# Full-height products and spread-by-transposition in a hybrid encoder block on one core

## The chip, the core and the metric

One NeuronCore of one Trainium2 chip runs the whole program; the other cores are idle. The metric is the time of one execution on the device in microseconds (us), as the median of repeated runs. PE is TensorE, DVE is VectorE, ACT is ScalarE, POOL is GpSimd, SP is the queue from which nearly all DMAs are issued.

## The reference, cut to what matters

One encoder layer over 16 meta tokens and 512 tokens of width 1024, in float32:

```
u    = rms_norm(h);  proj = u @ w_in              # r,k,v | low-rank wd, ad, gd | q,k,v | gates A, B
A:   z = centred_shift(p);  decay = exp(-exp(-softplus(-(w0 + tanh(wd) @ w2)) - 0.5))
     a = sigmoid(a0 + ad @ a2);  g = sigmoid(gd) @ g2
     kk = (k * k_k) / max(norm(k * k_k per head), 1e-12)          # "key norm"
     scan per direction: S = S*w + (S @ -kk) x (kk*a) + v x k';  y = S @ r
     y = group_norm(y per head) * lnx_g + lnx_b + bonus;  out = y * g   # "group norm"
B:   grouped attention: softmax(q_norm_rope @ k_norm_rope) @ v
h   += (sigmoid(A) * (y_a @ wba) + sigmoid(B) * (y_b @ wbb)) @ w_out
h   += relu(rms_norm(h) @ w_ff1)^2 @ w_ff2;   out = rms_norm(h)
```

## The kernel before

Activations lie with channels on the 128 partitions and tokens along the row. A float32 product is usually made of three products of rounded pieces: `mm3` (lines 132 to 134) multiplies hi with hi, hi with lo and lo with hi, where hi is the value rounded to the faster product format and lo the rest. Weights come by `wblock` (lines 121 to 128): a DMA of 512 KB, a cast on ACT (`whi`), a subtraction on DVE (`wlo`).

The stages, in order of time: (1) up to 75 us, the projections of the low-rank inputs, the normalisation of the tokens and of the attention's keys; (2) 75 to 152 us, the queries (lines 132 to 134 into `mm`), the tables of decay, in-context rate and gate for all head pairs (lines 498 to 549, the `rw` banks), and the first r,k,v projections (`project_rkv`, lines 191 and 192); (3) 155 to about 590 us, for four head pairs `hp`: preparation (`prepare`, which begins with `key_norm`), inversion of blocks (`invert`), the serial scan over nine chunks (`chain`) and `finish` with the group norm, with the rest of the projections and the gates as filler, and from about 443 us on the attention (`attend`) among them; (4) the branch projections, the output projection and the feed-forward part to the end.

The order of the instructions on each engine is drawn up at build time by a planner that simulates the program with its own costs (`schedule_with_timeline_sim=True`); `tc.issue_after` holds the stage of the tables behind a given product, and `run` mixes the parts of stage 3 by turns with a fixed pace of fillers. The engines then run their lists in that order. A change of operations can therefore change the order too.

Four kinds of place matter here.

- Products over fewer than 128 rows. The tables of decay and rate multiply a stacked operand (`wds[d]`, `ads[d]`: 64 rows of hi and 64 rows of lo) once with 128 rows of hi weights, `hh[d]` (lines 506 and 537), and then the 64 hi rows with 64 rows of lo weights (lines 507 and 538). For the 16 meta tokens lines 525 and 526 multiply plain float32 operands over 16 and 64 rows. Line 598 spreads the key norm of the meta tokens over 16 rows. Line 1078 adds the meta tokens' part of the attention's output over 48 rows, once for each half of the queries of each head. Line 546 is the gate's last product, over 96 rows.
- Spreads. A factor per token lies along the partitions and is needed along the row: it is copied to a full 128x128 tile (`rx`) and multiplied with the identity, in plain float32. Each such product stands as two PE records in the trace. This is done for the token norm (line 269, and 272 for the meta tokens), for the key norm (603) and the group norm (920) of each head pair, and for the norm before the feed-forward part (1223), four products of 128 columns each time. The attention's probabilities are turned by `pe.transpose` (line 1063), one record each.
- `constants()` (lines 304 to 327): casts on ACT and subtractions on POOL that make `hh`, `lo` and the gate's weights.
- The tile `sg` (line 508) in three buffers: DVE adds the bias (509), ACT applies the sigmoid (510) and casts (513), POOL subtracts (514). The one for the meta tokens (`i == 4`) is kept until the last product of line 525.

Of the kernel before, what the change touches and what calls it, by code (L numbers as in the profile page):

```python
# [7 lines left out]
F32R = mybir.dt.float32r  # L8
# [6 lines left out]
P = 128  # L15
# [34 lines left out]
def block_kernel(tc, A, out, dbg=None):  # L50
# [34 lines left out]
    with root:  # L85
# [20 lines left out]
        DC_C0, DC_KKH, DC_KAH, DC_KAB, DC_A0H, DC_RKH = 0, 16, 20, 24, 28, 0  # L106
        tmpc = T(cp, [P, 16])
        rkh = T(cp, [P, 4])
# [42 lines left out]
        with ph1:  # L151
# [22 lines left out]
            def whole(steps):  # L174
                while True:
                    try:
                        next(steps)
                    except StopIteration as e:
                        return e.value
# [46 lines left out]
            with ExitStack() as es:  # L226
# [15 lines left out]
                sy.dma_start(cst, A["cst"])  # L242
                ps12 = whole(project_steps(first, raw))
                g.tensor_tensor(tmpc, par[:, PC_MU0:PC_MU0 + 16], par[:, PC_MU1:PC_MU1 + 16], op=ALU.add)
                g.tensor_scalar(der[:, 0:16], tmpc, -1.0, 1.0, op0=ALU.mult, op1=ALU.add)
# [22 lines left out]
                for i in range(4):  # L268
                    pe.matmul(ps[:, i * P:(i + 1) * P], rx[:, i], ident, start=True, stop=True)
                s.copy(RT[:, NM:L], ps)  # L270
                ps = T(chp, [P, 512], tag="yp", bufs=1)
                pe.matmul(ps[:, 0:NM], rx[:, 4], ident[:, 0:NM], start=True, stop=True)
                s.copy(RT[:, 0:NM], ps[:, 0:NM])
# [31 lines left out]
                def constants():  # L305

                    c = {}
                    trr = T(wpy, [P, 2, P], F32R)
                    g.tensor_copy(trr, tri)
                    c["tri"] = trr  # L310
                    for n, t in (("w2", w2), ("a2", a2)):
                        hh = [T(wpy, [P, 512], F32R) for _ in range(2)]
                        lo = T(wpy, [P, 512], F32R)
                        for d in range(2):
                            for o in (d, 1 - d):
                                s.copy(hh[d][HF[o]], t[HF[d]])
                            g.tensor_tensor(lo[HF[d]], t[HF[d]], hh[d][HF[d]], op=ALU.subtract)
                        c[n] = hh, lo
                    gh, gl = T(wpy, [P, 512], F32R), T(wpy, [P, 512], F32R)
                    s.copy(gh, gw0)  # L320
                    g.tensor_tensor(gl, gw0, gh, op=ALU.subtract)
                    gs = T(wpy, [96, 512], F32R)
                    for x in (0, 2):
                        s.copy(gs[32 * x:32 * x + 32], gw1)
                    v.tensor_tensor(gs[32:64], gw1, gs[0:32], op=ALU.subtract)
                    c["gw"] = gh, gl, gs
                    return c
# [159 lines left out]
                v.tensor_tensor(sl, sgd0, sh, op=ALU.subtract)  # L487
                sst = T(wpz, [96, SEQ], F32R)
                for x in range(2):
                    s.copy(sst[32 * x:32 * x + 32], sgd1)  # L490
                v.tensor_tensor(sst[64:96], sgd1, sst[0:32], op=ALU.subtract)
                keys_values(tk_, qkg, identr)
# [5 lines left out]
                with tc.issue_after(started):  # L498
                    sgs = {}
                    for d in range(2):  # L500
                        for i in range(4 if d else 5):
# [4 lines left out]
                            pe.matmul(ps[0:n, :], wds[d][:, c - 48:c - 48 + n], hh[d], start=True, stop=False)  # L506
                            pe.matmul(ps[0:n, :], wds[d][HF[d], c - 48:c - 48 + n], lo[HF[d]], start=False, stop=True)
                            sg = T(wpy, [P, 512], tag="sg", bufs=3)
                            v.tensor_tensor(sg[0:n, :], ps[0:n, :], w0b[0:n, d, :], op=ALU.add)
# [7 lines left out]
                    for d in range(2):  # L517
                        for hp in range(NHP):
# [4 lines left out]
                            if d == 0:  # L523
                                pm = bank()
                                pe.matmul(pm[:, 0:NM], sgs[0, 4][0:NM, hc], tri[0:NM, 0, 0:NM], start=True, stop=True)
                                pe.matmul(pm[:, 16:32], a2[0:64, hc], adz[0:64, 48:64], start=True, stop=True)
                                v.tensor_copy(lo_[:, 0, 0:NM], pm[:, 0:NM])
                                s.activation(lo_[:, 1, 0:NM], pm[:, 16:32], AF.Tanh, scale=0.5, bias=ab)
# [8 lines left out]
                            pe.matmul(ps, hh[d][:, hc], ads[d][:, NM:L], start=True, stop=False)  # L537
                            pe.matmul(ps, lo[HF[d], hc], ads[d][HF[d], NM:L], start=False, stop=True)
                            s.activation(lo_[:, 1, NM:L], ps, AF.Tanh, scale=0.5, bias=ab)
# [13 lines left out]
            gtp = pool(ph1a, "gt1", side="right")  # L553
            rp = pool(ph1, "rw")
            def load_rkv(hp):
                zs = []
                for x in range(3):
                    z = T(zp, [P, 576], tag="z", bufs=ZB)
                    g.memset(z[:, 0:48], 0.0)
                    sy.dma_start(z[:, 48:576], z_d[hp, x])  # L560
                    zs.append(z)
                return zs
# [14 lines left out]
            def key_norm(hp, zk):  # L577
# [13 lines left out]
                rx = G()  # L591
                rxm = T(rp, [NM, P], tag="rxm", bufs=1)
                v.tensor_copy(rx[:, 0:512].rearrange("p (a b) -> p a b", b=64), rn[:, 0:8].unsqueeze(2).broadcast_to([P, 8, 64]))
                v.tensor_copy(rxm.rearrange("p (a b) -> p a b", b=64), rn[0:NM, 8:10].unsqueeze(2).broadcast_to([NM, 2, 64]))
                kkh = G("k")
                g.memset(kkh[:, 0:48], 0.0)
                ps = bank()
                pe.matmul(ps[:, 0:NM], rxm, ident[0:NM, 0:NM], start=True, stop=True)
                v.scalar_tensor_tensor(kkh[:, 48:64], zk[:, 48:64], dcol(DC_KKH + hp), ps[:, 0:NM],
                                       op0=ALU.mult, op1=ALU.mult)  # L600
                ps = bank()
                for i in range(4):
                    pe.matmul(ps[:, i * P:(i + 1) * P], rx[:, i * P:(i + 1) * P], ident, start=True, stop=True)
                v.scalar_tensor_tensor(kkh[:, 64:576], zk[:, 64:576], dcol(DC_KKH + hp), ps,
# [293 lines left out]
            def finish(hp, sh):  # L898
# [20 lines left out]
                for i in range(4):  # L919
                    pe.matmul(ps[:, i * P:(i + 1) * P], rx[:, i * P:(i + 1) * P], ident, start=True, stop=True)  # L920
                yield
# [99 lines left out]

            vm = T(ap_, [48, 2, P], F32R)
            pms = [T(ap_, [48, 256], F32R) for _ in range(2)]
            for part, t in ((0, khh), (1, kll)):
# [3 lines left out]
            lpp = pool(aes, "aloop", side="right")  # L1028
            zz = T(lpp, [P, 256], tag="yo", bufs=2)[0:48]
            g.memset(zz, 0.0)  # L1030
# [102 lines left out]
        with ExitStack() as es:  # L1133
# [88 lines left out]
            for i in range(4):  # L1222
                pe.matmul(ps[:, i * P:(i + 1) * P], rx[:, i, :], ident, start=True, stop=True)
            s.copy(RS, ps)
# [152 lines left out]
```

## Time and profile before

| | |
|---|---|
| time, median of 3 runs | 1050.72 us (1048.79 to 1052.95) |
| the profiled execution, its own time | 1051.4 us |
| span in its profile | 1049.6 us |
| PE busy / weight loads (PEld) | 994.9 us (95%) / 816.1 us (78%) |
| DVE / ACT / POOL busy | 592.2 (56%) / 434.4 (41%) / 185.9 us (18%) |
| granted PE clock, mean | 0.968 of full speed |
| DMA | 107.25 MB, mean 102 GB/s |

The span is the profiled stretch; about 1.8 us of that execution's time lie outside it. Busy shares are averages over very different stages. A PE record lasts longer than the step from its start to the next record's start, since products overlap in the array; what a product costs the stream is read from starts.

### The profile page before, as it was taken

To read this page: it belongs to the slowest core of one execution; us is meant where nothing else is said; L and a number is where in the kernel's file an instruction comes from. 1 tells how busy PE (TensorE), PEld (TensorE's weight loads), DVE (VectorE), ACT (ScalarE), POOL (GpSimd) and SP (SyncE) were. 2 spreads that over 40 slices of the span, in tenths; PEclk is the share of its full clock that TensorE was granted. 3 is DMA by queue.
4 is the path that set the end of the run, shared out by engine and by line. 5 is a ranking of instruction groups with operands and counts; after the bars stand their busy time and mean duration, and the time that the engine had idled before them with its cause. 6 is when DMAs were issued, how large, how long until landed. Compare 5 with 4: busy or idle time off the path is not lost.

```text
span 1049.6 us, 17962 instructions
## 1 busy us (share of the span) xinstructions
PE 994.9 (95%) x7208; PEld 816.1 (78%) x7208; DVE 592.2 (56%) x1084; ACT 434.4 (41%) x802; POOL 185.9 (18%) x373
## 2 busy tenths in 40 slices
PE   7799989989999899989989999999999999999996
PEld 7778978877767676767777788888888888888885
DVE  4967647756663737396977566455555552123123
ACT  6676434424322524275788533343332232113112
POOL 1266411411411132112311123000000000001001
PEclk9999999999989899886999999999999999999999
DMA  9233662232222211510010284222233332322322
GB/s 348 70 113 86 197 239 71 72 117 100 80 93 92 82 62 62 174 42 11 12 32 21 82 269 132 83 86 95 98 101 101 101 109 92 101 92 89 101 96 85
DMA packets 45508, 107.25 MB, mean 102 GB/s; under 512 B 5264, under 2 KB 12736, under 8 KB 45424
## 3 DMA queue, kind: packets, MB, share of 16 engines
q1 hardware_dynamic: 44848, 105.05, 30.7%
q8 instruction: 57, 0.93, 0.4%
q10 hardware_dynamic: 576, 1.05, 0.3%
q14 instruction: 27, 0.22, 0.1%
HBM read 87.54 MB, written 18.54 MB: 101 GB/s over the span
## 4 chain that ended last, share of the span: by engine, by line
PE 81%; DVE 10%; ACT 4%; issue 2%; DMA 2%; POOL 0%; SPq 0%; ACTq 0%; DVEq 0%; POOLq 0%
PE f L134 8%; PE f L133 8%; PE f L132 8%; PE t L132 6%; PE t L133 6%; PE t L134 6%; PE mm L132 5%; PE mm L133 4%; PE mm L134 4%; PE mm L191 4%; PE mm L192 3%; PE rw L705 2%; PE rw L813 2%; PE yp L869 1%; PE xu L847 1%
## 5 line engine op out<-in xcount | busy, mean ns | idle before, releaser
L126 ACT CAST whi<-wraw 128x1024 fp32r<-128x1024 f32 x118 | 123.7, 1050 | 321.9 <-PE f L134 76.8
L127 DVE TENSOR_TENSOR wlo<-wraw,whi 128x1024 fp32r<-128x1024 f32 x118 | 148.6, 1260 | 183.8 <-ACT whi L126 183.4
L191 PE MATMUL mm<-t,whi 128*128 128x264 f32 x240 | 70.0, 309 | 7.6 <-ACT t L239 7.5
L132 PE MATMUL f<-t,whi 128*128 128x512 f32 x184 | 72.0, 392 | 0.0
L133 PE MATMUL f<-t,whi 128*128 128x512 f32 x184 | 71.7, 390 | 0.0
L134 PE MATMUL f<-t,wlo 128*128 128x512 f32 x184 | 70.9, 390 | 0.0
L192 PE MATMUL mm<-t,whi 128*128 128x264 f32 x240 | 67.7, 299 | 0.0
L133 PE MATMUL t<-wlo,t 128*128 128x512 f32 x160 | 63.4, 396 | 0.0
L133 PE MATMUL f<-wlo,t 128*128 128x512 f32 x160 | 63.3, 396 | 0.0
L134 PE MATMUL f<-whi,t 128*128 128x512 f32 x160 | 63.3, 396 | 0.0
L134 PE MATMUL t<-whi,t 128*128 128x512 f32 x160 | 63.3, 395 | 0.0
L132 PE MATMUL mm<-t,whi 128*128 128x512 f32 x128 | 58.1, 454 | 0.0
L191 PEld LDWEIGHTS mm<-t,whi 128*128 128x128 f32 x240 | 47.9, 199 | 10.8 <-ACT t L239 7.5
L132 PE MATMUL t<-whi,t 128*128 128x512 f32 x160 | 54.7, 397 | 0.0
L132 PE MATMUL f<-whi,t 128*128 128x512 f32 x160 | 53.9, 395 | 0.0
L132 PE MATMUL t<-t,whi 128*128 128x512 f32 x136 | 53.2, 393 | 0.2 <-ACT whi L126 0.2
L134 PE MATMUL t<-t,wlo 128*128 128x512 f32 x136 | 53.0, 391 | 0.0
L133 PE MATMUL t<-t,whi 128*128 128x512 f32 x136 | 52.6, 389 | 0.0
L133 PE MATMUL mm<-t,whi 128*128 128x512 f32 x128 | 52.2, 408 | 0.0
L134 PE MATMUL mm<-t,wlo 128*128 128x512 f32 x128 | 52.0, 406 | 0.0
L1266 POOL TENSOR_TENSOR t<-t,t 128x512 f32<-128x512 f32 x4 | 5.1, 1302 | 261.0 <-DVE t L1263 261.0
L192 PEld LDWEIGHTS mm<-t,whi 128*128 128x128 f32 x240 | 47.9, 200 | 1.5 <-issue 1.4
(338 smaller groups left out, 2372.6 us busy)
## 6 DMA issues: line engine op xcount, KB each, us to landing
wraw<-in_w SPq DMA_DIRECT2D x32, 512.0 KB, 3.4
wraw<-in_w2f SPq DMA_DIRECT2D x32, 512.0 KB, 3.4
wraw<-in_wrk SPq DMA_DIRECT2D x16, 512.0 KB, 3.9
wraw<-in_wg SPq DMA_DIRECT2D x16, 512.0 KB, 3.7
t<-gt SPq DMA_DIRECT2D x16, 256.0 KB, 2.0
gt<-t SPq DMA_DIRECT2D x16, 256.0 KB, 3.3
wraw<-in_wo SPq DMA_DIRECT2D x8, 512.0 KB, 3.4
g<-t SPq DMA_DIRECT2D x12, 256.0 KB, 3.4
```

Of the source, the lines that this page charges most:

```text
L126: s.copy(hi, raw)
L127: v.tensor_tensor(lo, raw, hi, op=ALU.subtract)
L132: pe.matmul(o, ah, bh, start=first, stop=False)
L133: pe.matmul(o, ah, bl, start=False, stop=False)
L134: pe.matmul(o, al, bh, start=False, stop=last)
L191: pe.matmul(pa, wt[:, w], ut[:, k, 0:264], start=first, stop=last)
L192: pe.matmul(pb, wt[:, w], ut[:, k, 264:528], start=first, stop=last)
L705: pe.matmul(ps[:, c - a, :, :], bkh(h, c), xr[HR[h], h:h + 2, c, :], start=True, stop=True)
L813: pe.matmul(ps[HR[h], cc], hs[HR[h], cc], cur[HR[h], cc], start=True, stop=True)
L847: pe.matmul(X[HR[h], j], ps[d]["xr"][:, 2 * h, c, :], svu[:, c, h, :], start=True, stop=True)
L869: pe.matmul(yp[HR[h], j], svu[:, c, h, :], ps[d]["rl"][:, h, c, :], start=False, stop=last and j == 1)
L1266: (v if half else g).tensor_tensor(o[:, i, cols], h1[:, i, cols], fg[:, cols], op=ALU.mult)
```

## The change

Every product with fewer than 128 rows on the lines above gets 128: `lo` is kept twice (a tile for each direction, both halves filled by a further ACT copy), so lines 507 and 538 multiply the whole stacked operand; `gs` and `sst` get a second lo part (one more DVE subtraction each); `sg` of the meta tokens and `rxm` are cleared first, so that lines 525 and 598 run over 128 rows; line 526 becomes two products in the rounded format over the stacked operand; `vm` and `pms` of the attention get 128 rows, cleared below the used ones. `sg` has two buffers in place of three. The products with the identity over 128 rows become transpositions. `tmpc` moves to another pool.

```
-        tmpc = T(cp, [P, 16])
...
+                tmpc = T(xp, [P, 16])
...
-                    pe.matmul(ps[:, i * P:(i + 1) * P], rx[:, i], ident, start=True, stop=True)
+                    pe.transpose(ps[:, i * P:(i + 1) * P], rx[:, i], ident)
...
-                pe.matmul(ps[:, 0:NM], rx[:, 4], ident[:, 0:NM], start=True, stop=True)
+                pe.transpose(ps[:, 0:P], rx[:, 4], ident)
...
-                        lo = T(wpy, [P, 512], F32R)
+                        lo = [T(wpy, [P, 512], F32R) for _ in range(2)]
                         for d in range(2):
                             for o in (d, 1 - d):
                                 s.copy(hh[d][HF[o]], t[HF[d]])
-                            g.tensor_tensor(lo[HF[d]], t[HF[d]], hh[d][HF[d]], op=ALU.subtract)
+                            g.tensor_tensor(lo[d][HF[d]], t[HF[d]], hh[d][HF[d]], op=ALU.subtract)
+                            s.copy(lo[d][HF[1 - d]], lo[d][HF[d]])
...
-                    gs = T(wpy, [96, 512], F32R)
+                    gs = T(wpy, [P, 512], F32R)
                     for x in (0, 2):
                         s.copy(gs[32 * x:32 * x + 32], gw1)
-                    v.tensor_tensor(gs[32:64], gw1, gs[0:32], op=ALU.subtract)
+                        v.tensor_tensor(gs[32 * x + 32:32 * x + 64], gw1, gs[0:32], op=ALU.subtract)
...
-                sst = T(wpz, [96, SEQ], F32R)
+                sst = T(wpz, [P, SEQ], F32R)
                 for x in range(2):
                     s.copy(sst[32 * x:32 * x + 32], sgd1)
-                v.tensor_tensor(sst[64:96], sgd1, sst[0:32], op=ALU.subtract)
+                    v.tensor_tensor(sst[64 + 32 * x:96 + 32 * x], sgd1, sst[0:32], op=ALU.subtract)
...
-                            pe.matmul(ps[0:n, :], wds[d][HF[d], c - 48:c - 48 + n], lo[HF[d]], start=False, stop=True)
-                            sg = T(wpy, [P, 512], tag="sg", bufs=3)
+                            pe.matmul(ps[0:n, :], wds[d][:, c - 48:c - 48 + n], lo[d], start=False, stop=True)
+                            sg = T(wpy, [P, 512], tag="sg", bufs=2)
+                            if i == 4:
+                                g.memset(sg, 0.0)
...
-                                pe.matmul(pm[:, 0:NM], sgs[0, 4][0:NM, hc], tri[0:NM, 0, 0:NM], start=True, stop=True)
-                                pe.matmul(pm[:, 16:32], a2[0:64, hc], adz[0:64, 48:64], start=True, stop=True)
+                                pe.matmul(pm[:, 0:NM], sgs[0, 4][:, hc], tri[:, 0, 0:NM], start=True, stop=True)
+                                for x in range(2):
+                                    pe.matmul(pm[:, 16:32], con["a2"][x][0][:, hc], ads[0][:, 0:NM], start=x == 0, stop=x == 1)
...
-                            pe.matmul(ps, lo[HF[d], hc], ads[d][HF[d], NM:L], start=False, stop=True)
+                            pe.matmul(ps, lo[d][:, hc], ads[d][:, NM:L], start=False, stop=True)
...
+            rxm = T(rp, [P, P])
+            g.memset(rxm, 0.0)
...
-                pe.matmul(ps[:, 0:NM], rxm, ident[0:NM, 0:NM], start=True, stop=True)
+                pe.matmul(ps[:, 0:NM], rxm, ident[:, 0:NM], start=True, stop=True)
...
-                    pe.matmul(ps[:, i * P:(i + 1) * P], rx[:, i * P:(i + 1) * P], ident, start=True, stop=True)
+                    pe.transpose(ps[:, i * P:(i + 1) * P], rx[:, i * P:(i + 1) * P], ident)
...
-            vm = T(ap_, [48, 2, P], F32R)
-            pms = [T(ap_, [48, 256], F32R) for _ in range(2)]
+            vm = T(ap_, [P, 2, P], F32R)
+            pms = [T(ap_, [P, 256], F32R) for _ in range(2)]
...
-            zz = T(lpp, [P, 256], tag="yo", bufs=2)[0:48]
+            zz = T(lpp, [P, 256], tag="yo", bufs=2)
...
-                pe.matmul(ps[:, i * P:(i + 1) * P], rx[:, i, :], ident, start=True, stop=True)
+                pe.transpose(ps[:, i * P:(i + 1) * P], rx[:, i, :], ident)
```

The pair of lines with `rx[:, i * P:(i + 1) * P]` stands twice in the diff, in `key_norm` and in `finish`; the last pair is that of the norm before the feed-forward part.

## Rows read from the trace of the kernel before

**Rows 1.** The page: PE's part of the busy line, and the chain that ended last.

```profile
PE 994.9 (95%) x7208; PEld 816.1 (78%) x7208; DVE 592.2 (56%) x1084; ACT 434.4 (41%) x802; POOL 185.9 (18%) x373
...
PE 81%; DVE 10%; ACT 4%; issue 2%; DMA 2%; POOL 0%; SPq 0%; ACTq 0%; DVEq 0%; POOLq 0%
```

**Rows 2.** Stretches: length, busy time (instructions) by engine, granted clock, DMA share, GB/s.

```profile
130.00:155.00 25.00, 22.47 (x146) 18.67 (x145) 10.53 (x16) 8.80 (x12) 2.64 (x11) 0.97 0.71 244
...
450.00:525.00 75.00, 67.60 (x694) 53.87 (x692) 63.33 (x160) 50.63 (x123) 19.07 (x48) 0.86 0.08 23
525.00:610.00 85.00, 80.54 (x857) 65.33 (x857) 57.36 (x125) 57.39 (x133) 14.23 (x16) 1.00 0.19 60
300.00:310.00 10.00, 7.92 (x80) 6.34 (x81) 7.17 (x23) 2.65 (x5) 0.80 (x6) 0.69 0.23 79
```

**Rows 3.** Timeline of PE: start, length, line, rows*columns, the moving operand.

```profile
76.06 0.40 PE L506 MATMUL rw<-t,t 128*128 128x512 f32 x1
76.38 0.50 PE L507 MATMUL rw<-t,t 64*128 64x512 f32 x1
76.81 0.49 PE L506 MATMUL rw<-t,t 128*128 128x512 f32 x1
```

**Rows 4.** Timeline of PE at the gate's product.

```profile
146.06 0.40 PE L546 MATMUL rw<-t,t 96*128 96x512 f32 x1
146.29 0.39 PE L132 MATMUL rw<-t,t 128*128 128x512 f32 x1
```

**Rows 5.** Timeline of PE at short products for the meta tokens, in two places.

```profile
101.56 0.28 PE L192 MATMUL mm<-t,wlo 128*128 128x264 f32 x1
101.77 0.39 PE L525 MATMUL rw<-t,sg 16*128 16x16 f32 x2
...
102.41 0.36 PE L415 MATMUL xu<-identr,qp 128*128 128x128 f32 x2
...
23.63 0.29 PE L272 MATMUL yp<-t,t 128*128 128x16 f32 x2
23.77 0.37 PE L191 MATMUL rw<-t,wlo 128*128 128x264 f32 x1
```

**Rows 6.** Timeline of PE at the end of an attention half.

```profile
590.37 0.28 PE L1076 MATMUL tp<-pth,t 128*128 128x256 f32 x1
590.48 0.28 PE L1077 MATMUL tp<-ptl,t 128*128 128x256 f32 x1
590.69 0.38 PE L1078 MATMUL tp<-t,t 48*128 48x256 f32 x1
591.00 0.70 PE L904 MATMUL rw<-g,t 128*128 128x512 f32 x1
```

**Rows 7.** Timeline of PE at transpositions and spreads, in two places.

```profile
553.81 0.60 PE L1063 MATMUL tp<-t,pb 128*128 128x128 f32 x4
554.25 1.06 PE L920 MATMUL rw<-t,g 128*128 128x128 f32 x8
555.14 0.38 PE L1071 MATMUL tp<-t,pb 128*16 128x128 f32 x2
...
156.87 2.08 PE L603 MATMUL rw<-t,g 128*128 128x128 f32 x8
158.60 0.57 PE L191 MATMUL mm<-t,whi 128*128 128x264 f32 x1
```

**Rows 8.** Timeline of ACT and DVE around the constants.

```profile
66.75 5.09 ACT L316 CAST t<-t 64x512 fp32r<-64x512 f32 x8
...
74.75 1.23 DVE L127 TENSOR_TENSOR wlo<-wraw,whi 128x1024 fp32r<-128x1024 f32 x1 [1.04 <-ACT whi L126]
```

**Rows 9.** Timeline: one decay tile on DVE and POOL.

```profile
98.19 0.67 DVE L509 TENSOR_TENSOR sg<-rw,t 128x512 f32<-128x512 f32 x1
...
100.26 1.42 POOL L514 TENSOR_TENSOR sgl<-sg,sgh 128x512 fp32r<-128x512 f32 x1 [0.28 <-ACT sgh L513]
```

**Rows 10.** Timeline of DVE near the end of the second stage.

```profile
151.41 0.69 DVE L548 COPY gg<-rw 128x512 f32<-128x512 f32 x1 [2.53 <-DMA t<-gg]
```

More of the change, by code (lines that the diff above doesn't have):

```diff
@@ L591, in key_norm @@
                 rx = G()
-                rxm = T(rp, [NM, P], tag="rxm", bufs=1)
                 v.tensor_copy(rx[:, 0:512].rearrange("p (a b) -> p a b", b=64), rn[:, 0:8].unsqueeze(2).broadcast_to([P, 8, 64]))
-                v.tensor_copy(rxm.rearrange("p (a b) -> p a b", b=64), rn[0:NM, 8:10].unsqueeze(2).broadcast_to([NM, 2, 64]))
+                v.tensor_copy(rxm[0:NM].rearrange("p (a b) -> p a b", b=64), rn[0:NM, 8:10].unsqueeze(2).broadcast_to([NM, 2, 64]))
                 kkh = G("k")
@@ L919, in finish @@
                 for i in range(4):
-                    pe.matmul(ps[:, i * P:(i + 1) * P], rx[:, i * P:(i + 1) * P], ident, start=True, stop=True)
+                    pe.transpose(ps[:, i * P:(i + 1) * P], rx[:, i * P:(i + 1) * P], ident)
                 yield
```

## The prediction

> **What bounds the kernel now.** I read the page first. PE is busy 95% of the span, and the chain that ended last runs through PE for 81% of its length [rows 1]: work taken from PE is worth something in most places, but not everywhere in full. The table of stretches says where. From 130 to 155 us PE still has 22.47 of 25 us, but the DMA engines are at 0.71, and near the end of that stretch DVE waits 2.53 us for a DMA of the gate's table, with the next key norm's bank behind it [rows 2, 10]. From 450 to 525 us DVE has 63.33 of 75 us and PE waits between its steps; from 525 to 610 us PE has 80.54 of 85 us [rows 2]. After 610 us PE is the only bound. Last I read the timeline of PE, by the steps between starts, around each kind of place that the change touches. What a record lasts says little there: a record of 0.40 us can be followed by the next after 0.23 us [rows 4].
>
> **Products of fewer rows.** A 128-row product is followed by a 64-row one after 0.32 us (76.06 to 76.38), and that by the next 128-row product after 0.43 us (76.38 to 76.81) [rows 3]. With 96 rows and the same 512 columns the step is 0.23 us (146.06 to 146.29) [rows 4]. So a 64-row product between 128-row ones costs 0.75 - 2 x 0.23 = 0.29 us beyond its columns: some of it on the product ahead of it, the rest on itself. The trace shows the exposed time and not its cause; that 96 rows pay nothing says that it isn't the mere number of unused rows. The change makes these products 128 high with the same columns, so I take 0.29 us off each. There are 9 of them at line 507 (one with 16 weight columns: about 0.19) and 8 at line 538: 2.5 + 2.3 = 4.8 us.
>
> The Trainium skill, "TensorE: Matmul & The Clock Gate", section "Why this matters for your kernels", says that a single matmul of 32 rows takes as long as one of 128. By that rule the 4.8 us, and the other terms from row counts below, would be zero. Here the trace disagrees: 0.43 against 0.23 us for the same 512 columns [rows 3, 4].
>
> Line 1078, with 48 rows: the steps are 0.11 us between 128-row products of 256 columns, 0.21 us into the 48-row one and 0.31 us out of it [rows 6], so 0.52 - 0.22 = 0.30 us. It stands 16 times; 13 are followed by a 128-row product, 3 by 64-row ones, which will still have to be entered after the change (I give those 0.1 us). 13 x 0.30 + 0.3 = 4.2 us.
>
> Lines 525 and 526: from the last product before them to the first after them 0.85 us (101.56 to 102.41) [rows 5]. With 128 rows, two records of 16 columns take 0.14 us together (23.63 to 23.77) [rows 5]; line 526 is two products before and after. So 0.12 + 0.14 + about 0.16 = 0.42 us, 0.4 less, four times: 1.6 us. Line 598 has the form of line 525, which the same rows price at 0.32 us (a good part of 0.85) against 0.14, plus the step into it: about 0.3 us each, four times, 1.2 us.
>
> **Spreads by transposition.** Four transpositions at line 1063 take 0.44 us to the next start (553.81 to 554.25); the four float32 products of line 920 right behind them stand as eight records and take 0.89 us (554.25 to 555.14) [rows 7]. One record is left for two, so 0.45 us less per spread at full clock, and double where the granted clock is at its half level, where eight records took 1.73 us (156.87 to 158.60) [rows 7]. Ten spreads change: one before 25 us, four key norms, four group norms and the one before the feed-forward part. Two of the key norms run at half clock now: 8 x 0.45 + 2 x 0.9 = 5.4 us. The meta tokens' spread at line 272 goes from two records of 16 columns to one of 128, a wash.
>
> The Trainium skill, same page, section "Part 4: PE-mode transpose", holds that transpositions don't release the clock as matmuls do. It would turn the gain around (a rival below). The attention speaks against it as a strong effect: with four transpositions at line 1063 in each block of queries, 525 to 610 us has a granted clock of 1.00 [rows 2].
>
> **What is added.** Four more casts on ACT of 64x512, 0.64 us each (eight take 5.09) [rows 8]: 2.6 us. They stand in a stretch where ACT has no gap, each behind a POOL subtraction, and the cast of the next weight block is queued behind them, for which DVE's `wlo` already waits 1.04 us [rows 8]. PE's cover is about one microsecond of table products, so nothing to 2.6 us of PE idle; I take 1.5, since the cover is near but short. One more DVE subtraction of 32 rows in `constants` fits in DVE's idle time there, and one in `sst` stands beside a saturated PE; without that cover each would be about 0.7 us (an add of the same 512 columns takes 0.67) [rows 9]. The clearing of `sg`, `rxm`, `vm` and `pms` is POOL and DVE work ahead of need; without cover, some tenths of a us each.
>
> `sg` loses a buffer, and one of the two left is kept by the meta tokens until line 525 is done. The four tiles of the second direction then go one after another: from the add at 98.19 to the end of the POOL subtraction at 101.68 is 3.5 us [rows 9], four make 14 us, against about 13 us that those four take now. Behind the waiting add stand a bank of `rw` and the products that want it; but the r,k,v projections fill PE there, and the second direction's tables are wanted much later. I take nothing; the other end is four times the 3.5 us less the 9.3 us over which the adds spread now: 4.7 us.
>
> **The sum.** PE has 4.8 + 4.2 + 1.6 + 1.2 + 5.4 = 17.2 us less work. By stage: 0.45 before 25 us, on the chain, in full. 75 to 152 us: 4.8 + 1.6 = 6.4, of which I pass 0.6, as PE is full there but the stretch ends in transfers that an earlier PE only crowds: 3.8. 155 to 600 us: 1.2 + 4.2, four key norms at 2.7 and three group norms at 1.35, 9.45 in all; with 81% of the whole chain on PE, but DVE ahead of it in the first half of the attention, I pass 0.6 again: 5.7. The group norm at 606 us and the last spread, 0.9, in full. 0.45 + 3.8 + 5.7 + 0.9 - 1.5 = 9.35 us. The profiled execution took 1051.4 us, so 1042.0; the median of the runs is 0.7 us lower, and I predict 1041 us. The bounds of the sum: everything passes and the casts are hidden, 1051.4 - 17.2 = 1034; nothing of the two middle stages passes and both added costs are paid, 1051.4 - 1.35 + 2.6 + 4.7 = 1057.
>
> **The rivals.**
>
> *Hidden anyway.* PE's savings turn into idle time: from 75 to 152 us the DMA queue sets the end (0.71 busy), from 155 to 600 us the serial scan and DVE do. For it: DVE's 63.33 of 75 us and the wait of 2.53 us [rows 2, 10]. Against: PE's 80.54 of 85 us and 81% of the chain. Only 0.45 + 0.9 and a little more are left: 1048 to 1050 us, no change.
>
> *Row counts buy nothing*, the skill's rule: the extra 0.29 us would belong to the operands and stay. Only the spreads count: 0.45 + 0.9 + 0.6 x 4.05 - 1.5 = 2.3 us, 1049 us. Against it stand the 0.23 us of the 96-row product and the 0.14 us of the two 128-row records [rows 4, 5].
>
> *The clock falls at the spreads* (slower). Seven spreads between 155 and 600 us go from 0.9 us of matmuls to 0.45 us of transpositions, which, if they don't hold the clock, come on top of a gap. A fall as at 300 to 310 us, behind a gap on PE, leaves 0.69 of the clock over 10 us, so some 3.1 us of clock [rows 2]. Seven such falls are 22 us: 1042 + 22 = 1064 us. Three use up the 9.35 us; from five on the kernel is over 0.5% slower (1042 + 15.5 = 1057).
>
> *The planner orders it otherwise.* Its costs for a transposition, a 128-row product and one free `sg` slot change every list behind them. The trace prices no new order; the nearest row is the 2.53 us wait, and a few such waits more or fewer move the forecast by up to some 8 us either way: 1034 to 1050 us, or, with the 4.7 us of `sg` in full and two falls of the clock, 1058 us.
>
> **How the numbers follow.** Less than 0.5% (5.25 us) can't be told from no change here. The forecast, 1034 to 1045.4 us, gets 0.56; hidden 0.22; row counts 0.03; the clock 0.07; another order 0.12, of which a third ends faster, a third the same and a third slower. Faster: 0.56 + 0.04 = 0.60. Same: 0.22 + 0.03 + 0.04 = 0.29. Slower: 0.07 + 0.04 = 0.11. The range, 1033 to 1053 us, takes in the forecast, hidden and row counts, half of the other orders, and leaves out most of the clock. The forecast's own range is 1034 to 1046.
>
> **What the profile would show.** Right: steps of 0.23 us at lines 507 and 538 and 0.12 us into and out of line 1078; four records in place of eight at lines 269, 603, 920 and 1223; PE's busy time some 15 us lower with idle time up by under 7; the key norm at 152 us reached 2 to 4 us earlier. Wrong if the 64-row steps were of the operands (no shorter steps), if PE's idle time grew by as much as its work fell, if POOL's `sgl` came to hold back PE at line 507, if ACT's casts let PE idle near 76 us, or if the granted clock of 155 to 525 us fell below its present values.

## The result and the profile after

The changed kernel took 1062.13 us (median of 18 runs, 1059.65 to 1068.67), the kernel before 1052.64 us in the same session: a ratio of 1.0091 (95% interval 1.0074 to 1.0109). It is 0.9% slower; 1041 us was predicted, and the range ended at 1053.

The profiled execution took 1061.26 us with a span of 1059.5 us and a mean granted clock of 0.956 (0.968 before). The page, its busy line and its chain, against [rows 1]:

```profile
PE 991.1 (94%) x7167; PEld 818.5 (77%) x7167; DVE 595.5 (56%) x1086; ACT 436.4 (41%) x806; POOL 187.1 (18%) x375
...
PE 76%; DVE 12%; ACT 4%; DMA 3%; issue 3%; POOL 1%; SPq 0%; ACTq 0%; DVEq 0%; POOLq 0%
```

PE is busy 3.8 us less by the page, not 15, and its share of the chain fell from 81% to 76%. The products themselves became shorter, as forecast. The timeline of PE, at lines 507 and 508 (506 and 507 before), at line 1083 (1078 before), and at the first key norm's spread:

```profile
82.04 0.40 PE L507 MATMUL rw<-t,t 128*128 128x512 f32 x1
82.27 0.40 PE L508 MATMUL rw<-t,t 128*128 128x512 f32 x1
82.51 0.40 PE L507 MATMUL rw<-t,t 128*128 128x512 f32 x1
...
577.07 0.28 PE L1082 MATMUL tp<-ptl,t 128*128 128x256 f32 x1
577.19 0.28 PE L1083 MATMUL tp<-t,t 128*128 128x256 f32 x1
577.30 0.28 PE L1058 MATMUL sc<-t,qs 128*128 128x264 f32 x1
...
153.24 0.63 PE L608 MATMUL rw<-t,g 128*128 128x128 f32 x4
153.63 0.36 PE L190 MATMUL mm<-t,whi 128*128 128x264 f32 x1
```

The steps are 0.23 us where 0.32 and 0.43 us stood [rows 3], 0.12 and 0.11 us where 0.21 and 0.31 us stood [rows 6], and four records in 0.39 us where eight took 0.89 us at full clock [rows 7]. This spread starts 3.6 us earlier than the one before (156.87) [rows 7].

The time is lost later. Stretches of the kernel after, in the columns of [rows 2]:

```profile
130.00:155.00 25.00, 20.45 (x125) 16.36 (x124) 11.11 (x20) 9.15 (x15) 4.06 (x16) 0.93 0.79 262
450.00:525.00 75.00, 69.15 (x605) 57.79 (x605) 58.67 (x141) 49.32 (x115) 20.73 (x53) 0.73 0.15 51
525.00:610.00 85.00, 79.40 (x996) 65.66 (x997) 63.08 (x154) 62.14 (x149) 13.73 (x19) 1.00 0.11 33
...
250.00:300.00 50.00, 45.41 (x370) 34.69 (x370) 32.67 (x89) 17.59 (x40) 13.12 (x42) 0.93 0.21 65
350.00:400.00 50.00, 41.20 (x347) 31.97 (x342) 27.08 (x55) 19.52 (x44) 10.57 (x27) 0.86 0.24 75
```

The kernel before, in the two of them that have no row ahead of the prediction:

```profile
250.00:300.00 50.00, 49.65 (x434) 38.20 (x435) 33.31 (x80) 20.06 (x44) 14.53 (x42) 1.00 0.31 99
350.00:400.00 50.00, 47.28 (x353) 36.90 (x354) 27.87 (x61) 18.80 (x40) 14.19 (x41) 0.90 0.28 91
```

From 250 to 300 us PE lost 4.2 us of busy time, from 350 to 400 us 6.1 us, in stretches that hold no product and no spread that the change touched. The waits of PE in the kernel after, from 250 to 300 us and from 340 to 375 us (total, times, longest), name the two largest gaps:

```profile
PE mm L131 <- ACT gt L945: 3.4, 1, 3.4
...
PE rw L710 <- DVE g L726: 5.6, 1, 5.6
```

The first is a matter of ACT's list. Timeline of ACT after:

```profile
280.49 1.33 ACT L751 ACTIVATE g<-uw,t 128x256 f32<-128x256 f32 x2 [4.40 <-POOL uw L577]
281.73 1.03 ACT L125 CAST whi<-wraw 128x1024 fp32r<-128x1024 f32 x1
282.67 1.07 ACT L945 ACTIVATE gt<-mm 128x512 f32<-128x512 f32 x2
```

ACT idled 4.40 us for a POOL result with a weight cast and two tanhs of the gates behind it in its list. In the kernel before, the same cast and tanhs stood ahead of these scalings (lines 126, 940 and 746 there):

```profile
276.34 1.04 ACT L126 CAST whi<-wraw 128x1024 fp32r<-128x1024 f32 x1 [1.61 <-PE mm L133]
277.29 1.08 ACT L940 ACTIVATE gt<-mm 128x512 f32<-128x512 f32 x2
...
290.56 1.36 ACT L746 ACTIVATE g<-uw,t 128x256 f32<-128x256 f32 x2
```

The second gap is a matter of SP's list. Timeline of SP and of ACT behind it, kernel after:

```profile
354.31 0.32 SPq L934 DMA_DIRECT2D t<-g  x1
361.40 0.32 SPq L946 DMA_DIRECT2D t<-gt  x1
362.16 0.33 SPq L122 DMA_DIRECT2D wraw<-in_wg  x1
362.59 0.42 SPq L648 DMA_DIRECT2D g<-t  x1
...
367.36 0.63 ACT L664 ACTIVATE ep<-g 128x512 f32<-128x512 f32 x1 [4.56 <-DMA g<-t]
```

and the kernel before:

```profile
349.12 0.32 SPq L929 DMA_DIRECT2D t<-g  x1
349.53 0.38 SPq L643 DMA_DIRECT2D g<-t  x1
```

The loads of the decay and theta rows for the second direction (lines 648 and 650, 643 and 645 before) stood right behind the store of `ya_d` (lines 934 and 929) before; after, a gate store that waits for a tanh, and a weight load, stand between, and the first leaves 8.3 us behind that store in place of 0.4. ACT waits 4.56 us for it, and PE for what ACT and DVE make of it.

Of PE's 5631 instructions that both kernels have, some 540 stand in another relative place, on DVE 192, on ACT 153, on SP 24. So my theory was: the changed products save what was counted, and the order that the planner drew up with them costs more. The rivals were that the saving is hidden anyway, and that the clock falls at the transpositions.

### The profile page after: what moved, and what is told of

Read it like the earlier page. It is cut to its first block, busy times and chain, and to the rows that moved or that the text cites. A ratio compares the mean times of both kernels' runs of the same rounds, so it can differ in the third digit from the quotient of the medians.

```text
span 1059.5 us, 17883 instructions
## 1 busy us (share of the span) xinstructions
PE 991.1 (94%) x7167; PEld 818.5 (77%) x7167; DVE 595.5 (56%) x1086; ACT 436.4 (41%) x806; POOL 187.1 (18%) x375
## 4 chain that ended last, share of the span: by engine, by line
PE 76%; DVE 12%; ACT 4%; DMA 3%; issue 3%; POOL 1%; SPq 0%; ACTq 0%; DVEq 0%; POOLq 0%
PE f L133 7%; PE f L132 7%; PE f L131 7%; PE t L131 6%; PE t L132 6%; PE t L133 6%; PE mm L131 5%; PE mm L132 4%; PE mm L133 4%; PE rw L710 3%; PE rw L818 2%; PE mm L190 2%; PE mm L191 2%; PE yp L874 1%; DMA g<-t 1%
## 5 line engine op out<-in xcount | busy, mean ns | idle before, releaser
L190 PEld LDWEIGHTS mm<-t,whi 128*128 128x128 f32 x240 | 48.1, 200 | 10.5 <-ACT t L238 6.9
L710 PE MATMUL rw<-xr,bk 64*128 64x128 f32 x272 | 44.6, 318 | 11.0 <-DVE g L726 7.9
```

The lines of the kernel that those rows point to most:

```text
L190: pe.matmul(pa, wt[:, w], ut[:, k, 0:264], start=first, stop=last)
L710: pe.matmul(ps[:, c - a, :, :], bkh(h, c), xr[HR[h], h:h + 2, c, :], start=True, stop=True)
```

## The experiments

Most of the runs fix the order, so that operations and order can be exchanged one for the other. A table gives each engine's list, and every instruction gets a dependency for order alone on the one ahead of it in its list:

```
+        pin_order(tc, nc)
...
+        order = [mine[k] for a, m in ORDER[n] for k in range(a, a + m)]
+        for a, b in zip(order, order[1:]):
+            tc.add_manual_dep(b, a.name, mybir.DependencyInfo(mybir.DependencyClass.NoSync, ...
```

In the two runs of the changed operations in the order of before, POOL's list is left to the planner; in the two runs of the operations of before in another order, DVE's is. No run gives a kernel its own order by such a table and changes nothing else; the nearest is the kernel before with one buffer less, at 1.0014 (below), so the added dependencies cost little.

Ratios are to the kernel before in the same session; each run has 5 to 12 executions. Differences between runs of different sessions are taken from the ratios, or, where it is said, from the medians.

### The changed operations in the order of before, and the reverse

Edit: `ORDER` holds the lists of the other kernel; the operations are those of the changed kernel in the first run and those of the kernel before in the second.

> All operations of the changed kernel, but each engine's list stands in the order of the kernel before (an instruction that only one of the two kernels has stands beside its neighbour). Order theory: the changed operations save work and the loss came from the order that the planner drew up, so this kernel is faster than before, 1035 to 1045 us; the 1.33 us of ACT work that stood behind a wait of 4.40 us near 280 us in the changed kernel is early again, and the stretch from 450 to 500 us has a granted clock near 0.80 as before and not 0.59. Rival, the saving is hidden: 1049 to 1054 us. Rival, the products themselves or the ten transpositions (as work that lets the clock fall) cost the time: 1057 to 1066 us, as the changed kernel.

Measured: 1051.24 us, ratio 0.9992 (0.9968 to 1.0015).

> All operations of the kernel before, but with the order of the changed kernel on PE, ACT, POOL and SP (DVE's list is left to the planner: 39 of its instructions stand otherwise). Order theory: this kernel has the loss without the saving, 1063 to 1077 us. Rivals by which the operations cost the time: 1049 to 1056 us, as the kernel before.

Measured: 1078.59 us, ratio 1.0269 (1.0230 to 1.0307).

The reverse is clear: the order of the changed kernel makes the operations of before 2.7% slower (DVE's list is not quite the same), so the operations don't cost the time. In that order they even save 1.0269 - 1.0091 = 1.78%, 18.7 us, more than the 17.2 us of work that were counted out. The first run missed my 1035 to 1045 us: the loss is gone, but so is the saving, as the rival "hidden" had it. Its trace shows where. Timeline of ACT and then of PE in that run:

```profile
73.53 0.62 ACT L318 CAST t<-t 64x512 fp32r<-64x512 f32 x1 [0.75 <-POOL t L317]
...
78.60 1.04 ACT L125 CAST whi<-wraw 128x1024 fp32r<-128x1024 f32 x1
...
79.70 0.50 PE L131 MATMUL mm<-whi,t 128*128 128x512 f32 x1 [3.40 <-ACT whi L125]
```

The order of before has no place for the four new copies of `lo` (line 318), so I had put each beside its neighbour. There each waits for POOL, POOL waits for ACT, the weight cast comes 4.9 us later than before, and PE waits 3.40 us. The values of the first pair (the products of line 617, line 622 with the changed operations, the first that need the finished projection of `v`) came at 164.0 us (161.1 before, 155.3 in the changed kernel). The prediction had priced just this, with nothing to 2.6 us; there was more to lose, since the copies wait besides costing their own time.

### Each half of the change, in the planner's own order

Edit of the first, at all ten spreads and at the meta tokens' one (line 272), and at no other line, one pair of five shown; the second is the changed kernel with these lines undone:

```
-                    pe.matmul(ps[:, i * P:(i + 1) * P], rx[:, i], ident, start=True, stop=True)
+                    pe.transpose(ps[:, i * P:(i + 1) * P], rx[:, i], ident)
```

> Only the ten spreads as transpositions (their records should halve, 0.89 to about 0.45 us each), with the row counts as before; the planner draws up its own order (255 of PE's instructions stand otherwise than before). Order theory: the sum of the work is 5 us smaller but the time may fall anywhere from 1043 to 1065 us, and where it differs from before by more than 5 us, the trace shows a wait of several us at a place that has no spread. Rival, the clock falls at the spreads: 1057 to 1066 us, with the granted clock lower in the stretches right behind the spreads (155, 606 and 645 us). Rival, hidden: 1049 to 1054 us.

Measured: 1061.52 us, ratio 1.0111 (1.0074 to 1.0147).

> Only the products of 128 rows, with the ten spreads as products with the identity as before; the planner draws up its own order (465 of PE's instructions stand otherwise than before). Order theory: the sum of the work is about 12 us smaller, the time may fall anywhere from 1040 to 1070 us. Rival, the clock falls at the spreads: at most 1046 us, since nothing but the saving is left. Rival, the longer operands (zeros and copies on ACT and POOL, the group's buffer with two places for three) cost the time: 1057 to 1066 us, with waits of PE for that buffer in the stretch from 75 to 150 us.

Measured: 1049.07 us, ratio 0.9967 (0.9948 to 0.9987).

Here "the clock falls at the spreads" looked as good as the order: all of the loss comes with the transpositions, although the second run missed that rival's 1046 us. But the run with the spreads alone has the loads late too. SP in the run with the spreads:

```profile
359.04 0.32 SPq L941 DMA_DIRECT2D t<-gt  x1
359.81 0.33 SPq L123 DMA_DIRECT2D wraw<-in_wg  x1
360.23 0.42 SPq L643 DMA_DIRECT2D g<-t  x1
```

and in the run with the row counts:

```profile
347.08 0.32 SPq L934 DMA_DIRECT2D t<-g  x1
347.49 0.38 SPq L648 DMA_DIRECT2D g<-t  x1
```

In the first PE waited 5.3 us at line 705 for what follows on these loads. At the place of the tanhs, near 280 us, it waited only 0.3 us, so that run shares one of the two late places with the changed kernel, and what else it lost isn't named. Fixing the order had to decide.

### The spreads alone, in the order of before

Edit: the lines above, with the lists of the kernel before.

> Only the ten spreads as transpositions, every engine's list in the order of the kernel before. Theory that the order alone cost the 10 us of the run with only the spreads: 1045 to 1050 us here (5.4 us less work on PE, of which some waits elsewhere). Rival, the clock falls at the spreads and that costs: 1055 to 1064 us, as with the free order, with a lower granted clock right behind 155, 606 and 645 us. Rival, the spreads are hidden: 1050 to 1053 us.

Measured: 1051.80 us, ratio 1.0002 (0.9978 to 1.0027). The 1.1% is gone with the order; the theory of the clock is refuted as the cause of it. But 5.4 us less work on PE bought nothing here either: the time missed my 1045 to 1050 us and lies where the rival "hidden" had it. The profiled execution shows one thing that eats such a gain. Stretch of this run, then of the kernel before:

```profile
170.00:200.00 30.00, 28.01 (x169) 24.85 (x167) 19.62 (x38) 10.43 (x22) 9.16 (x31) 0.78 0.20 68
```

```profile
170.00:200.00 30.00, 28.04 (x218) 24.84 (x217) 22.20 (x45) 12.18 (x25) 7.67 (x25) 1.00 0.26 84
```

PE is as busy and does 169 records in place of 218, because its clock fell to half for some 14 us from 187 us on, some 30 us behind the nearest spread. The values of the first pair were 1.8 us ahead there (159.3 against 161.1 us); the first product of line 862 starts at 213.5 us, 209.6 us before.

The other executions agree. The mean granted clock of each is on record, and span x (1 - clock) is an estimate of the time that the half clock added, if PE had work all the while. Its median is 39.9 us here and 34.6 in the kernel before of that session (clocks of 0.962 and 0.967); what is left of the span is 1008.9 and 1014.4 us. So about the 5.4 us that were counted were saved, and about as much went to a lower clock. Why the clock is lower isn't shown.

### The two late places, mended one by one in the changed kernel's own order

Edit of ACT's list in the first, SP's list in the second, both in the third:

```
 ACT, near 280 us
-  L751 x2 (scalings), L125 (weight cast), L945 x2 (tanhs)
+  L125 (weight cast), L945 x2 (tanhs), L751 x2 (scalings)
 SP, near 354 us
-  L934, L946 (gate store), L122 (weight load), L648, L650
+  L934, L648, L650, L946 (gate store), L122 (weight load)
```

> The changed kernel in its own order, but for one place of ACT's list: a cast of a weight tile and two tanhs of gates stand ahead of the two scalings of the substitution (280 us) in place of behind them. In the changed kernel ACT waited 4.40 us there, PE 3.4 us for a bank, and the granted clock fell near 283 us. Order theory: PE's wait near 283 us goes and the time falls by 3 to 7 us: 1055 to 1059 us. Rival, given back at the next wait, the loads at 362 us: 1060 to 1064 us.

Measured: 1055.49 us, ratio 1.0016 (0.9989 to 1.0043).

> The changed kernel in its own order, but for one place of SP's list: the two loads of the decay and theta rows for the second direction of the third pair (354 to 364 us) stand ahead of the gate store and the weight load, as in the kernel before. In the changed kernel the loads were issued at 362.59 us behind a store that waited for a tanh, and PE waited 5.6 us for what follows on them. Order theory: they are issued near 354.7 us, PE's wait of 5.6 us goes, and the time falls by 4 to 9 us: 1053 to 1058 us. Rival, this wait only shows what is late for another reason: 1060 to 1064 us.

Measured: 1059.30 us, ratio 1.0070 (1.0050 to 1.0089).

> The changed kernel in its own order but for the two places tried one by one: the cast and the tanhs ahead of the two scalings on ACT (280 us) and the two loads ahead of the gate store on SP (354 us). Theory that the two are separate losses: 1062.1 - 6.6 - 2.8 = 1052.7, range 1050 to 1055 us. Rival, one delay seen at two places: 1054 to 1058 us, no less than with the first alone (1055.5).

Measured: 1052.30 us, ratio 1.0000 (0.9977 to 1.0023).

Two instructions moved behind three others on ACT give back 6.6 us by the medians (0.75% by the ratios). ACT in that run:

```profile
279.67 1.04 ACT L125 CAST whi<-wraw 128x1024 fp32r<-128x1024 f32 x1 [2.45 <-PE mm L132]
280.62 1.08 ACT L945 ACTIVATE gt<-mm 128x512 f32<-128x512 f32 x2
282.71 1.40 ACT L751 ACTIVATE g<-uw,t 128x256 f32<-128x256 f32 x2 [1.01 <-POOL uw L577]
```

PE's wait of 3.4 us became 0.3 us, and the clock didn't fall behind it. From 283 to 289 us, changed kernel and then this run:

```profile
283.00:289.00 6.00, 5.69 (x13) 4.46 (x14) 4.55 (x18) 0.90 (x3) 0.00 (x0) 0.50 0.52 178
```

```profile
283.00:289.00 6.00, 6.00 (x33) 4.65 (x32) 5.20 (x21) 3.03 (x6) 2.15 (x5) 1.00 0.37 117
```

So a wait of 3.4 us cost about twice its length, and what the profile shows for the other half is the half clock behind it, some 6 us long. The starts of the tanhs (line 945) in the two profiles say the same: this run is 1.1 us behind the changed kernel at 241 us and 4.8 us ahead at 293 us. The loads, moved, left at 353.03 us, and PE's wait of 5.6 us became three of 2.2 us together:

```profile
353.03 0.38 SPq L648 DMA_DIRECT2D g<-t  x1
...
PE rw L710 <- DVE g L726: 2.2, 3, 1.0
```

That alone gives 2.8 us, less than the 4 us that I had as the least; by the intervals of the ratios (1.0050 to 1.0089 against 1.0074 to 1.0109) it can't be told from nothing. Together they give 9.8 us by the medians, where the sum of the two is 9.4, as forecast, though by the intervals that run can't be told from the one with the tanhs alone either. Here the profiles speak: by the starts of the same tanhs, 4.1 us are won between 361 and 394 us with the loads moved, and 4.4 and 4.5 us at the two places with both (the profiled execution with the loads moved is the shortest of its twelve, 1053.34 us). Two places, then; the second one's share in the times isn't certain.

### A mixed order

Edit: up to the first key norm (150 us) the lists of the changed kernel, behind it those of the kernel before; all operations are the changed ones.

> All operations of the changed kernel; up to the key norm of the first pair (150 us) each engine's list stands in the changed kernel's own order, behind it in the order of the kernel before. Theory: the order of the kernel before was drawn for three buffers sg, and with the two that the change leaves the run of all changed operations in that order lost its saving ahead of 164 us (values of the first pair at 164.0 us, 155.3 in the changed kernel); with the first part in its own order the values come near 155.3 and the rest takes what it took in that run (427 us to the last sum of 48 rows, 591.0): 1051.2 - 8.7 = 1042.5, range 1039 to 1046 us, faster than both kernels. Rival, what is won ahead of 155 us is given back later, because another wait ends last there: 1048 to 1053 us.

Measured: 1044.73 us, ratio 0.9934 (0.9909 to 0.9958): faster than both kernels. The values came at 156.5 us. With the same operations as the changed kernel the order alone makes 17.4 us by the medians (1.6% by the ratios), and since the lists up to 150 us are the changed kernel's own, what its order loses is lost behind them. The page's busy line of this run, and its stretch from 450 to 525 us:

```profile
PE 981.5 (94%) x7167; PEld 809.8 (78%) x7167; DVE 596.2 (57%) x1086; ACT 437.2 (42%) x806; POOL 188.5 (18%) x375
```

```profile
450.00:525.00 75.00, 65.48 (x729) 53.47 (x729) 64.51 (x163) 52.19 (x125) 19.94 (x50) 0.91 0.09 26
```

PE is busy 13.4 us less than in [rows 1], near the 15 us that were forecast, and the clock of 450 to 525 us is 0.91, with all ten transpositions in place, against 0.73 in the changed kernel's order and 0.86 before [rows 2].

### The change undone in that order, whole and in half

Edit: the diff undone, or only its ten transpositions, with the lists of the mixed order.

> The operations of the kernel before in the order that took 1044.7 us with the changed operations (18 of DVE's instructions stand otherwise). Theory that the changed operations save time once the order is the same: 1051 to 1062 us, that is 6 to 17 us more (17.2 us is the work counted out, 9.35 us what was said to be passed on). Rival, the order alone was good and the operations change nothing: 1043 to 1048 us.

Measured: 1054.94 us, ratio 1.0034 (1.0017 to 1.0050).

> The changed operations without the ten transpositions (the spreads again as products with the identity), in the order that took 1044.7 us with them. Theory that a part of the spreads' 5.4 us is passed on where PE has no wait: 1046 to 1050 us. Rival, the spreads are hidden: 1043 to 1046 us. Rival, the clock falls at the transpositions: 1036 to 1042 us.

Measured: 1046.35 us, ratio 0.9950 (0.9926 to 0.9973).

In one order, then, the change is worth 1.0034 - 0.9934 = 1.0%, 10.5 us, and most of it comes from the row counts: 1.0034 - 0.9950 = 0.84%, 8.8 us. The transpositions are left with 0.16%, 1.7 us, within the intervals; the second run lies on the border between passed on and hidden. (18 of DVE's instructions stand otherwise in the first of these runs.)

### What took the saving in the order of before

Two things were open: the buffer `sg` that the change takes away, and the place where I had put the four copies. First the kernel before with one edit, in its own order:

```
-                            sg = T(wpy, [P, 512], tag="sg", bufs=3)
+                            sg = T(wpy, [P, 512], tag="sg", bufs=2)
```

> The kernel before in its own order, but with two buffers sg in place of three. Theory that the lost buffer is what the order of the kernel before can't bear: waits of PE between 75 and 155 us, the values of the first pair at 165 to 170 us (161.1 before), 1053 to 1060 us. Rival, the stall up to 164 us in the run of the changed operations in that order came from the copies of lo that ACT has in addition: no new wait, values at 161 to 162.5 us, 1050 to 1053 us.

Measured: 1053.18 us, ratio 1.0014 (0.9986 to 1.0043). The time lies on the border of the two and can't tell them apart. But PE had no new wait for a buffer `sg` (its longest new one ahead of 155 us is 0.5 us, at line 415 for a cast on ACT), and the values came at 162.1 us: the rival's side, and my theory of the buffer fell for this kernel. Then the changed operations in the order of before again, with ACT's list mended:

```
 ACT, 67 to 78 us
-  L316 x2, L318, L316 x2, L318, L316 x2, L318, L316 x2, L318, L321, L325 x2, L125
+  L316 x8, L321, L325 x2, L125, L318 x4
```

> The changed operations in the order of the kernel before, as in the run that took 1051.2 us, but with the four new copies of lo on ACT behind the weight cast that followed them, where the changed kernel's own order has them too. In that run each of the four waited for POOL (0.75 to 0.99 us), the cast began at 78.60 us (73.66 in the kernel before) and PE waited 3.40 us for it. Theory that the place of these copies took the saving: the wait of 3.40 us goes, the values of the first pair come at 157 to 161 us (164.0 in that run) and the time is 1044 to 1048 us. Rival, the two buffers sg took it (DVE and ACT late between 80 and 110 us): values at 162 to 164 us, 1049 to 1053 us.

Measured: 1046.86 us, ratio 0.9946 (0.9929 to 0.9963). ACT in this run:

```profile
73.26 1.05 ACT L125 CAST whi<-wraw 128x1024 fp32r<-128x1024 f32 x1
74.33 2.55 ACT L318 CAST t<-t 64x512 fp32r<-64x512 f32 x4
```

The four copies run without a wait, PE's 3.40 us are gone, the values come at 159.2 us, and the changed operations are 0.54% faster than the kernel before in that kernel's own order.

The tile `sg` isn't free there, though. In this run, and in the one that took 1051.2 us, PE waits for `sg` at line 507, the first time because DVE waits for POOL to clear the tile of the meta tokens. DVE, and the sum of PE's waits:

```profile
92.11 0.68 DVE L512 TENSOR_TENSOR sg<-rw,t 16x512 f32<-16x512 f32 x1 [4.50 <-POOL sg L511]
...
PE rw L507 <- DVE sg L512: 2.5, 2, 1.4
```

What these 2.5 us cost in time was not tried.

## Why the prediction was wrong

**The step that failed** is the last rival, "the planner orders it otherwise". It said that the trace prices no new order, let "a few such waits more or fewer" move the forecast "by up to some 8 us either way", ended at 1058 us with two falls of the clock, and had a chance of 0.12, a third of it slower; the sum itself took the order at nothing. The order cost 17.4 us (1062.1 against 1044.7 us with the same operations; 15.3 us against the 1046.9 us of the order of before with the four copies behind the cast), more than the 10.5 us that the operations save in the mixed order, and put the time above the range. What was left out of its price: a wait of PE can be paid twice. DVE's 2.53 us [rows 10] were taken as the size of such a wait, where the two of PE that were followed up were 3.4 and 5.6 us, and the clock that falls behind a wait, which the prediction priced at 3.1 us for another rival, entered only at the slow end. By the estimate from the granted clocks the half clock took 47.6 us of the changed kernel and 37.5 us of the mixed order, and the rest of the span is 1012.6 and 1005.3 us: some 10 us of what the order cost are clock, some 7 are not.

**The products of fewer rows** were right: steps of 0.23 and 0.11 to 0.12 us, and 0.21 us into a 64-row product behind line 1083, the 0.1 us that was left to it. What was passed on came to 8.8 us in the mixed order. The prediction's share for them is 0.6 x (6.4 + 1.2 + 4.2) = 7.1 us less 1.5 for the copies on ACT, 5.6 us. By that order they were sized too low.

**The spreads** halved as counted (four records for eight, 0.39 us), but their part, 0.45 + 0.6 x (2.7 + 1.35) + 0.9 = 3.8 us, was sized too high: 1.7 us in the mixed order, nothing that can be measured in the order of before. The two errors cancel in the mixed order, where 10.5 us were measured and 9.35 forecast for the whole. That is luck: the same change was worth 5.7 us (0.54%) in the order of before with the copies mended, and 18.7 us (1.78%) in the changed kernel's order.

**The casts on ACT**, taken at 1.5 us, depend on their place: none of PE's waits came of them in the changed kernel's order, 3.40 us where they stood each behind POOL, against 2.6 us as the bound. **`sg`**, taken at nothing, cost at most 0.4% by the interval of its run; with the changed operations in the order of before PE waited 2.5 us for it.

**The rivals.** "Hidden anyway" was wrong in a fixed order with the copies in place. "Row counts buy nothing" was wrong. "The clock falls at the spreads" named a sign that came true, a lower granted clock (450 to 525 us: 0.73 against 0.86), but it isn't what made the kernel slower: with all ten transpositions it is 0.91 there in the mixed order and 0.86 in the order of before with the copies mended. A smaller loss did come with the transpositions in a fixed order, by the estimate from the clocks 5.3 us in the order of before and 3.0 us in the mixed one, against the 22 us of the rival; whether it is their doing isn't shown, since the one fall that was looked at stands 30 us behind a spread. **Busy time of PE** fell by 3.8 us and not by 15, since a record lasts longer at the lower clock: by the same estimate the clock took 13.0 us more than before, and 3.8 + 13.0 is near the 17.2 us that were counted. PE's idle time grew from 54.7 to 68.4 us, where under 7 us more had been the sign of being right. In the mixed order busy time fell by 13.4 us and idle time grew by 5.

**What stays open.** The two mended places give back 9.8 of the 17.4 us; the rest was not taken one by one. With the transpositions alone the planner drew an order that is 1.1% slower, with the row counts alone one that is 0.3% faster, so the transpositions tip it; which of its costs does so was not tried. Why the granted clock is lower with the transpositions in a fixed order is open.

## What to carry to other kernels

Where a planner draws up the lists, compare two kernels in one fixed order before judging an edit: here the same edit was +0.9% in the new order and -0.5, -1.0 and -1.8% in three fixed ones, so the saving too depends on the order. Price an in-order queue by what stands behind the instruction that waits: two instructions moved on ACT gave 6.6 us, four copies 4.4. And count a wait of PE with the clock behind it.

## What the runs showed of the hardware

The clock can fall without a visible cause in the change: with the spreads alone in the order of before, the granted clock was 0.78 from 170 to 200 us where the kernel before has 1.00, with the same busy time of PE (28.01 and 28.04 us). In the 12 us ahead of the fall, from 175 to 187 us, PE was busy 10.3 us in both.

The times of one kernel go with its granted clock. The twelve of that run lie from 1047.90 us (0.965) to 1056.65 us (0.954), those with the tanhs ahead from 1045.69 us (0.968) to 1058.74 us (0.959), and those of the kernel before beside them from 1047.96 us (0.970) to 1057.53 us (0.960). That the clock makes the difference in time, and doesn't only go with it, is argued.
